# HGRN2 in a hybrid encoder: scores for the diagonal 32x32 chunks alone, and both heads' value and state products ordered by block

## The chip, the cores and the metric

The kernel runs on one core of one Trainium2 chip. The metric is the device time of one execution in microseconds (us). TensorE (PE in the profile) multiplies matrices, and loads its weights on a sequencer of its own (PEld); VectorE is DVE, ScalarE is ACT, GpSimd is POOL, and SyncE (SP) issues most DMAs. Each engine works through its own list of instructions in order and waits on semaphores of the others.

## The reference

Two layers of an encoder over 512 tokens of width 1024. A layer normalizes, projects once, runs four mixers on column groups of the projection (Hyena, Mamba2, dilated attention, HGRN2), projects out, and ends in a mixture of 16 experts. The change is in HGRN2, which runs once per direction e (forward, backward), four heads of 64 channels each, in chunks of 32 tokens:

```python
def gla_chunked(q, k, v, g):
    q, k, v, g = rs(q), rs(k), rs(v), rs(g)             # (batch, chunk, 32, head, channel)
    gc = jnp.cumsum(g, axis=2)
    ref = gc[:, :, H_CHUNK // 2 - 1:H_CHUNK // 2]
    scores = jnp.einsum("bclhe,bcshe->bchls", q * jnp.exp(gc - ref), k * jnp.exp(ref - gc))
    scores = jnp.where(jnp.tril(jnp.ones((32, 32), bool)), scores, 0.0)
    o_intra = jnp.einsum("bchls,bcshp->bclhp", scores, v)
    U = jnp.einsum("bclhe,bclhp->bchep", k * jnp.exp(g_last - gc), v)
    _, prev = lax.scan(step, S0, (U, a))                # S = a * S + U, chunk by chunk
    o_inter = jnp.einsum("bclhe,bchep->bclhp", q * jnp.exp(gc), prev)
    return o_intra + o_inter
```

So a token meets only the tokens of its own chunk through a score, and all earlier chunks through the state `prev`. With 512 tokens there are 16 chunks, hence 16 blocks of 32x32 scores per head and direction.

## The kernel before

A layer's mixers are Python generators. `weave` (L428) advances two of them by turns, in proportion to the numbers that they yield, and so makes the program order; from that order a scheduler sets each engine's list when the program is built. In each layer `hgrn` is woven with `mamba_proj` (L584): while HGRN2 waits for a vector engine, TensorE does the projection of the Mamba mixer, `pcm` (128x128 weights, 512 columns, L395 to L397) and `ptm` (L417 to L419).

`hgrn` (L1119) works on heads in pairs: i is the pair, h the head in it, and head h's 64 channels lie on partitions 64h to 64h+63. For a pair, `hgrn_decay` makes the decayed keys and queries `gqk` and the decayed queries for the states `gqi`, for both directions e. Then, per direction, keys are transposed (`gkT`, L1135), multiplied with the values (`gU`, L1143, 64x64 weights), copied by ACT (L1148, L1150), and VectorE runs the scan over the 16 chunks (`gR`, L1153 or L1155, 128x1024).

Then comes the part that the change touches, per head h:

- Scores. For each direction four products of 128x128 (L1164): the tokens are taken 128 at a time (block b), though only the four 32x32 blocks on the diagonal are wanted. Weights have 64 rows and 128 columns.
- Mask. GpSimd clears a tile `gP` (L1166, 128x512), VectorE copies the wanted elements into it under a mask (`copy_predicated`, L1167, 128x512). After both directions VectorE adds the two tiles (L1170).
- Products. Per block b one product of the masked scores with the values (L1173, 128x128 weights, 64 columns), and then, for each chunk cc of the block and each direction, one product of decayed queries with the state (L1180, weights of 64 rows and 32 columns, 64 moving columns). All accumulate in the PSUM bank `go` of that head: `pov[h][:, b, i]`, chunk cc on partitions 32cc to 32cc+31.

A product of float32 operands leaves two records in the trace (two passes, each with its own load of weights). Per pair that makes 16 score products (32 passes), 8 value products (16 passes) and 60 state products (120 passes); there are two pairs in each of two layers.

After both pairs: squares on ACT (`gsq`, L1189), sums on VectorE (`gss`, L1190), the norm, a transposition on TensorE (`gyT`, L1202).

Of the kernel before, what the change touches and what calls it, by code (L numbers as in the profile page):

```python
# [20 lines left out]
P = 128  # L21
# [17 lines left out]
def shape_constants():  # L39
    f32 = np.float32  # L40
    p = np.arange(P)
    c = np.zeros((P, C_N), f32)
    c[:, C_ID:C_ID + P] = np.eye(P)
    c[:, C_LE:C_LE + P] = p[:, None] <= p[None, :]
    c[:, C_GE:C_GE + P] = p[:, None] >= p[None, :]
    c[:, C_IOTA:C_IOTA + 64] = np.arange(1, 65)
    c[:, C_TOK:C_TOK + 4] = 2 * (P * np.arange(4)[None, :] + p[:, None])
    c[:, C_HALF] = p >= 64
    c[:, C_KEY] = 1.0 / KEY
    c[:, C_KEY + 1] = 1.0  # L50
    c[:, C_SLOT] = p % 64 + 1
    same = (p[:, None] // 32) == (p[None, :] // 32)
    m = np.zeros((P, 2, P), np.int32)
    m[:, 0] = same & (p[:, None] <= p[None, :])
    m[:, 1] = same & (p[:, None] >= p[None, :])

    eo = np.concatenate([np.arange(0, L, 2), np.arange(1, L, 2)])
    f = 2.0 * np.pi * (np.arange(P, dtype=np.float64) + 0.5) / (2 * L)  # L60
    n = np.arange(L).reshape(P, 4).T
    th = n[:, :, None] * f
    dft = np.stack([np.cos(th), np.sin(th)]).astype(f32)
    idft = np.ascontiguousarray(dft.transpose(0, 1, 3, 2))
    tk = [eo[:, None] * f, eo[:, None] * (np.pi / 2 - f)]
    kdft = np.stack([np.concatenate([np.cos(tk[0]), np.cos(tk[1])], axis=1),
                     np.concatenate([np.sin(tk[0]), -np.sin(tk[1])], axis=1)])
    kdft = (kdft * (2.0 / (2 * L))).astype(f32)

    t = np.linspace(0.0, 1.0, L, dtype=f32)[:, None]  # L70
    ang_pos = (f32(2.0 * math.pi) * np.arange(L, dtype=f32) / f32(L)).astype(f32)
    bands = np.linspace(1e-4, 15, 16, dtype=f32)
    ang = (ang_pos[:, None] * bands[None, :]).astype(f32)
    z = np.concatenate([t, np.cos(ang), -np.sin(ang)], axis=-1).astype(f32)
    lo = math.log(1e-2) / 1.5
    hi = math.log(1e-2) / 0.3
    deltas = np.abs(np.linspace(lo, hi, 256, dtype=f32))
    decay = np.exp(-t * deltas[None, :]).astype(f32)[eo]

    d = np.arange(511, -512, -1)  # L80
    n = np.abs(d)
    nf = np.maximum(n, 1).astype(f32)
    large = 8 + (np.log(nf / f32(8)) / f32(math.log(128.0)) * f32(8)).astype(np.int32)
    bucket = (d > 0) * 16 + np.where(n < 8, n, np.minimum(large, 15))
    mult = (n <= 64).astype(int) + ((n <= 256) & (n % 4 == 0)) + (n % 16 == 0)
    oh = np.zeros((33, 1024), f32)
    oh[bucket, np.arange(1023)] = 1.0
    oh[32, :1023] = np.where(mult > 0, np.log(np.maximum(mult, 1)), -1e30)
    return {
        "c_pack": c, "c_hmask": m, "c_dft": dft, "c_idft": idft, "c_kdft": kdft,  # L90
        "c_zT": np.ascontiguousarray(z.T), "c_decay": decay, "c_bucket": oh,
    }
# [18 lines left out]
def encoder(ctx: ExitStack, tc: tile.TileContext, d, out, dbg=None, stages=None, nlayers=NL):  # L111
# [35 lines left out]
    def bank_b(name):  # L147
        return tagged(psb, "b", [512], F32, name)
# [71 lines left out]
    ps = bank_b("nmT")  # L220
# [898 lines left out]
    def hgrn(l, st, cols, lb):  # L1119
# [9 lines left out]
        for i in range(2):  # L1129
            qk, qi, bes = yield from hgrn_decay(l, i, q, f, lb, keep)  # L1130
            R = [tl("B", [64, 16], "gR") for _ in range(2)]
            for e in range(2):
                ps = bank_b("gkT")
                for b in range(4):
                    T.transpose(ps[:, b * P:(b + 1) * P], qk[1][:, e, b * P:(b + 1) * P], ident)  # L1135
                kT = page([4, P], "gkT")
                A.activation(kT, ps.rearrange("p (b c) -> p b c", b=4), AF.Copy)
                pu = [bank_b("gU") for _ in range(2)]
                for b in range(4):
                    for z in range(2):  # L1140
                        a = slice(64 * z, 64 * z + 64)
                        for h in range(2):
                            T.matmul(pu[z][64 * h:64 * h + 64, b * P:(b + 1) * P], kT[a, b, 64 * h:64 * h + 64],  # L1143
                                     ve[b][a, 2 * i + h], start=True, stop=True)

                U, w = tl("B", [64, 16], "gU"), tl("B", [64, 16], "gw")
                for z in range(2):
                    A.activation(U.rearrange("p n (b z c) -> p z b c n", z=2, c=2)[:, z],  # L1148
                                 pu[z].rearrange("p (b c n) -> p b c n", b=4, n=64), AF.Copy)
                A.activation(w, bes[e][:, None, :].to_broadcast([P, 64, 16]), AF.Copy)  # L1150
                u, r, w = (x.rearrange("p n c -> p (n c)") for x in (U, R[e], w))
                if e == 0:
                    V.tensor_tensor_scan(r, w, u, 0.0, ALU.mult, ALU.add)  # L1153
                else:
                    V.tensor_tensor_scan(r[:, ::-1], w[:, ::-1], u[:, ::-1], 0.0, ALU.mult, ALU.add)  # L1155
                yield 2.5
            for h in range(2):
                s = slice(64 * h, 64 * h + 64)
                Ps = []
                for e in range(2):  # L1160
                    ps = bank_b("gsc")
                    for b in range(4):
                        c = slice(b * P, (b + 1) * P)
                        T.matmul(ps[:, c], qk[1][s, e, c], qk[0][s, e, c], start=True, stop=True)  # L1164
                    w = page([4, P], "gP")
                    G.memset(w, 0.0)  # L1166
                    V.copy_predicated(w, hmask[:, e, None, :].to_broadcast([P, 4, P]),  # L1167
                                      ps.rearrange("p (b c) -> p b c", b=4))
                    Ps.append(w)
                V.tensor_add(Ps[0], Ps[0], Ps[1])  # L1170
                yield 2
                for b in range(4):
                    T.matmul(pov[h][:, b, i], Ps[0][:, b], v[:, b, (2 * i + h) * 64:(2 * i + h + 1) * 64],  # L1173
                             start=True, stop=False)
                    for cc in range(4):
                        c = 4 * b + cc
                        for e in range(2):
                            p = c - 1 if e == 0 else c + 1
                            if 0 <= p < 16:
                                T.matmul(pov[h][32 * cc:32 * cc + 32, b, i], qi[s, e, 32 * c:32 * c + 32],  # L1180
                                         R[e][s, :, p], start=False, stop=(e == 1 or c == 15))
                    yield 0.8
        gs = tl("B", [4, 256], "ggs")
        silu_inplace(g, gs, gs)
        y = tl("B", [4, 256], "gy")
# [457 lines left out]
```

## Time and profile before

| | before |
|---|---|
| runs, us (median of 3) | 1653.99 (1653.51 to 1654.05) |
| profiled execution, us | 1657.14 |
| its span, first to last instruction, us | 1655.4 |
| PE busy | 1531.7 us, 93% of the span |
| DVE busy | 802.6 us, 48% |
| ACT busy | 396.1 us, 24% |
| POOL busy | 213.8 us, 13% |
| mean granted TensorE clock | 0.971 |

All times in rows are in us from the start of the span, unless marked ns. The profiled execution lies 3.15 us above the median of the runs. `hgrn` of layer 0 fills the stretch from about 102 to 183 us, that of layer 1 from about 920 to 995 us. Matmuls are pipelined, so the rate of a burst is read from starts: a row of the timeline merges like instructions, its start is that of the first and its length ends with the last one's modelled end.

### The profile page before, as it was taken

What the parts mean: (1) busy time and instruction counts of PE and PEld (TensorE: products, weight loads), DVE (VectorE), ACT (ScalarE), POOL (GpSimd) and SP (SyncE); (2) the same over time, 40 slices, a digit from 0 to 9 for tenths busy, and PEclk for the clock granted to TensorE, in tenths of its full rate; (3) what the DMA queues carried; (4) which work ended last, traced back from release to release, by engine and by line L of the source; (5) the groups of instructions that cost most, each with busy time, mean ns of one, the idle gap of its engine ahead of it and who ended that gap; (6) DMA issues with size and microseconds to landing.
All of it is one profiled execution on the core that took longest, in us unless ns stands there. A gap on an engine that the chain in (4) does not pass through costs nothing.

```text
span 1655.4 us, 22757 instructions
## 1 busy us (share of the span) xinstructions
PE 1531.7 (93%) x8899; PEld 880.2 (53%) x8899; DVE 802.6 (48%) x1727; ACT 396.1 (24%) x805; POOL 213.8 (13%) x214
## 2 busy tenths in 40 slices
PE   6989998989999998989979999999899999998985
PEld 5778787763433432334368788787434433332332
DVE  6777677573333331432256767856533333332323
ACT  4344333431000000001162435243200001000012
POOL 3232133000000000000033232310000000000001
PEclk9989899999999999999989889999899999999998
DMA  5411223679999999999932202167799999999996
GB/s 169 127 51 36 68 77 141 239 288 341 421 420 421 421 420 399 421 420 420 419 95 82 72 27 77 54 233 266 262 407 418 420 422 420 421 420 421 420 420 247
DMA packets 153773, 468.54 MB, mean 283 GB/s; under 512 B 20440, under 2 KB 56696, under 8 KB 144962
## 3 DMA queue, kind: packets, MB, share of 16 engines
q1 hardware_dynamic: 145030, 455.10, 70.3%
q0 software_dynamic: 2240, 7.34, 1.1%
q10 hardware_dynamic: 6396, 4.65, 0.8%
q8 instruction: 70, 1.15, 0.3%
q14 instruction: 37, 0.30, 0.0%
HBM read 460.60 MB, written 6.44 MB: 282 GB/s over the span
## 4 chain that ended last, share of the span: by engine, by line
PE 63%; DMA 25%; DVE 6%; ACT 3%; issue 2%; POOL 1%; ACTq 0%; SPq 0%; DVEq 0%; POOLq 0%
PE eg L1404 9%; DMA we<-in_moe_w_up_dram 9%; DMA we<-in_moe_w_down_dram 9%; PE eu L1404 8%; PE ey L1404 7%; DMA we<-in_moe_w_gate_dram 5%; PE pcm L395 3%; PE pcm L396 3%; PE pcm L397 3%; PE ec L1475 2%; PE po L1222 2%; PE po L1223 2%; PE po L1224 2%; PE ptm L418 2%; PE ptm L417 2%
## 5 line engine op out<-in xcount | busy, mean ns | idle before, releaser
L1404 PE MATMUL eu<-we,exT 128*64 128x512 f32 x1024 | 237.9, 598 | 17.2 <-DMA we<-in_moe_w_up_dram 14.9
L1404 PE MATMUL ey<-we,ehT 128*64 128x512 f32 x1024 | 233.1, 600 | 17.3 <-ACT ehT L1440 11.2
L1404 PE MATMUL eg<-we,exT 128*64 128x512 f32 x1024 | 230.7, 598 | 10.4 <-DMA we<-in_moe_w_gate_dram 6.4
L1404 PEld LDWEIGHTS eu<-we,exT 128*64 128x64 f32 x1024 | 67.7, 136 | 181.6 <-issue 91.9
L1303 DVE SCALAR_TENSOR_TENSOR ra<-er,ra,tie 128x512 bf16<-128x512 f32 x128 | 95.9, 749 | 128.6 <-PE er L1311 125.7
L1404 PEld LDWEIGHTS ey<-we,ehT 128*64 128x64 f32 x1024 | 70.2, 137 | 155.5 <-issue 102.1
L1404 PEld LDWEIGHTS eg<-we,exT 128*64 128x64 f32 x1024 | 69.2, 136 | 149.6 <-issue 111.5
L1457 DVE SCALAR_TENSOR_TENSOR eY<-ey,erg,eY 64x512 fp32r<-64x512 f32 x64 | 48.0, 750 | 189.2 <-ACT eY L1456 189.1
L1425 ACT ACTIVATE eh<-eg 128x512 f32<-128x512 f32 x32 | 19.1, 598 | 498.6 <-PE eg L1404 498.6
L397 PE MATMUL pcm<-hT,whl 128*128 128x512 f32 x320 | 128.9, 403 | 3.5 <-DVE whl L381 3.5
L1476 DVE TENSOR_TENSOR x<-x,ec 128x512 f32<-128x512 f32 x128 | 81.0, 691 | 102.6 <-PE ec L1475 102.5
L396 PE MATMUL pcm<-hT,whl 128*128 128x512 f32 x320 | 130.2, 407 | 0.0
L395 PE MATMUL pcm<-hT,whl 128*128 128x512 f32 x320 | 129.9, 406 | 0.0
L1348 POOL DMA_INDIRECT exe<-xd,erow x28 | 27.8, 994 | 787.0 <-DVE erg L1329 660.1
L1456 ACT ACTIVATE eY<-ey,erg 64x512 fp32r<-64x512 f32 x64 | 43.7, 683 | 268.3 <-PE ey L1404 243.9
L1432 DVE TENSOR_TENSOR eh<-eh,eu 128x512 f32<-128x512 f32 x32 | 22.0, 687 | 153.9 <-PE eu L1404 153.9
L417 PE MATMUL ptm<-wtm,hT 128*128 128x256 f32 (+1 forms) x256 | 76.1, 298 | 1.7 <-DVE aqs L926 1.7
L1475 PE MATMUL ec<-eY,eot 128*128 128x512 f32 x256 | 67.3, 405 | 10.2 <-DVE erow L1346 6.4
L418 PE MATMUL ptm<-wtm,hT 128*128 128x256 f32 (+1 forms) x256 | 74.2, 291 | 1.3 <-DVE wtm L381 1.3
L380 POOL TENSOR_SCALAR whl<-wraw 128x1024 fp32r<-128x1024 f32 x40 | 46.9, 1173 | 220.1 <-PE pcm L397 127.7
L419 PE MATMUL ptm<-wtm,hT 128*128 128x256 f32 (+1 forms) x256 | 72.8, 288 | 0.0
L397 PEld LDWEIGHTS pcm<-hT,whl 128*128 128x128 f32 x320 | 62.3, 195 | 18.2 <-DVE whl L381 3.9
(394 smaller groups left out, 2374.8 us busy)
## 6 DMA issues: line engine op xcount, KB each, us to landing
we<-in_moe_w_gate_dram SPq DMA_DIRECT2D x218, 512.0 KB
we<-in_moe_w_up_dram SPq DMA_DIRECT2D x208, 512.0 KB
we<-in_moe_w_down_dram SPq DMA_DIRECT2D x206, 512.0 KB
wraw<-in_w_in_dram SPq DMA_DIRECT2D x27, 1024.0 KB
we<-in_moe_w_down_dram SPq DMA_DIRECT2D x25, 1024.0 KB
we<-in_moe_w_up_dram SPq DMA_DIRECT2D x24, 1024.0 KB
we<-in_moe_w_gate_dram SPq DMA_DIRECT2D x19, 1024.0 KB
wo<-in_w_out_dram SPq DMA_DIRECT2D x8, 1024.0 KB
```

Of the source, the lines that this page charges most:

```text
L380: G.tensor_scalar(dst_hi, raw, 1.0, 0.0, op0=ALU.mult, op1=ALU.add)
L395: T.matmul(ps, w[:, 0, k, :], H[k], start=(k == 0), stop=False)
L396: T.matmul(ps, w[:, 0, k, :], Lo[k], start=False, stop=False)
L397: T.matmul(ps, w[:, 1, k, :], H[k], start=False, stop=(k == 7))
L417: T.matmul(dst, h, w[:, 0, k % 4], start=(k == 0), stop=False)
L418: T.matmul(dst, h, w[:, 1, k % 4], start=False, stop=False)
L419: T.matmul(dst, g, w[:, 0, k % 4], start=False, stop=(k == 7))
L1303: V.scalar_tensor_tensor(g, pr, ra[:, c, e, 0:1], tie[:, 384 - c * P:896 - c * P], op0=ALU.subtract, op1=ALU.is_gt, accum_out=k)
L1404: T.matmul(ps[f][64 * f:64 * f + 64], xT[:, j, h], qs[4 * h + j][:, f * 512:(f + 1) * 512], start=(h == 0 and j == 0), stop=(h == 1 and j ...
L1457: V.scalar_tensor_tensor(lo, src, w[c, 0:1], hi.bitcast(F32), op0=ALU.mult, op1=ALU.subtract)
L1475: T.matmul(ps, ot[:, t * P:(t + 1) * P], Y[i][q][n], start=(q == 0), stop=(q == 1))
L1476: V.tensor_add(xrow(t)[:, c], xrow(t)[:, c], ps)
```

## The change

In the mask constant both directions now hold one 32x32 triangle, repeated for four column blocks and four row blocks. `hgrn` takes both heads of a pair together:

```diff
@@ shape_constants @@
-    same = (p[:, None] // 32) == (p[None, :] // 32)
-    m = np.zeros((P, 2, P), np.int32)
-    m[:, 0] = same & (p[:, None] <= p[None, :])
-    m[:, 1] = same & (p[:, None] >= p[None, :])
+    m = np.zeros((P, 2, 4, 32), np.int32)
+    m[:, 0] = ((p % 32)[:, None] <= np.arange(32))[:, None]
+    m[:, 1] = ((p % 32)[:, None] >= np.arange(32))[:, None]
+    m = m.reshape(P, 2, P)
@@ hgrn @@
+            pc = [bank_b("gsc") for _ in range(2)]
+            for e in range(2):
+                for c in range(16):
+                    b, cc = divmod(c, 4)
+                    t = slice(32 * c, 32 * c + 32)
+                    for h in range(2):
+                        s = slice(64 * h, 64 * h + 64)
+                        T.matmul(pc[h][32 * cc:32 * cc + 32, P * e + 32 * b:P * e + 32 * b + 32], qk[1][s, e, t],
+                                 qk[0][s, e, t], start=True, stop=True)
+            w = page([2, 2, P], "gP")
+            G.memset(w, 0.0)
             for h in range(2):
-                s = slice(64 * h, 64 * h + 64)
-                Ps = []
-                for e in range(2):
-                    ps = bank_b("gsc")
-                    for b in range(4):
-                        c = slice(b * P, (b + 1) * P)
-                        T.matmul(ps[:, c], qk[1][s, e, c], qk[0][s, e, c], start=True, stop=True)
-                    w = page([4, P], "gP")
-                    G.memset(w, 0.0)
-                    V.copy_predicated(w, hmask[:, e, None, :].to_broadcast([P, 4, P]),
-                                      ps.rearrange("p (b c) -> p b c", b=4))
-                    Ps.append(w)
-                V.tensor_add(Ps[0], Ps[0], Ps[1])
-                yield 2
-                for b in range(4):
-                    T.matmul(pov[h][:, b, i], Ps[0][:, b], v[:, b, (2 * i + h) * 64:(2 * i + h + 1) * 64],
-                             start=True, stop=False)
+                V.copy_predicated(w[:, h], hmask, pc[h][:, :256].rearrange("p (e c) -> p e c", e=2))
+            V.tensor_add(w[:, :, 0], w[:, :, 0], w[:, :, 1])
+            yield 3
+            for b in range(4):
+                for h in range(2):
+                    for cc in range(4):
+                        t = slice(32 * cc, 32 * cc + 32)
+                        T.matmul(pov[h][t, b, i], w[t, h, 0, 32 * b:32 * b + 32],
+                                 v[t, b, (2 * i + h) * 64:(2 * i + h + 1) * 64], start=True, stop=False)
+                for h in range(2):
+                    s = slice(64 * h, 64 * h + 64)
                     for cc in range(4):
...
-                    yield 0.8
+                yield 1.2
```

Per pair there are now 64 score products (weights of 64 rows and 32 columns, 32 moving columns; 128 passes), 32 value products (32x32 weights, 64 columns; 64 passes), and the same 60 state products (120 passes). VectorE has two masked copies of 128x256 and one addition of 128x256 in place of four copies and two additions of 128x512; GpSimd clears one tile of 128x512 in place of four.

TensorE's list in layer 0, pair 0, before. `gU` ends the chunk products, `gsc` are scores, `pcm` is the Mamba projection, `go` takes values (from `gv`) and states (from `gR`):

```order
L1143 MATMUL gU_1079<-gve_895,gkT_1076 64x128 x2
L1164 MATMUL gsc_1102<-gqk_956,gqk_957 128x128 x4
L1164 MATMUL gsc_1110<-gqk_956,gqk_957 128x128 x4
L396 MATMUL pcm_1125<-hT_127,whl_1122 128x512
...
L1173 MATMUL go_954<-gv_260,gP_1107 128x64
L1164 MATMUL gsc_1195<-gqk_956,gqk_957 128x128 x3
L1180 MATMUL go_954<-gR_1039,gqi_958 32x64
L1180 MATMUL go_954<-gR_1038,gqi_958 32x64
...
L1173 MATMUL go_954<-gv_260,gP_1107 128x64
L1180 MATMUL go_954<-gR_1038,gqi_958 32x64
```

The same place after the change:

```order
L1143 MATMUL gU_1079<-gve_895,gkT_1076 64x128 x2
L1165 MATMUL gsc_1102<-gqk_956,gqk_957 32x32
L1165 MATMUL gsc_1103<-gqk_956,gqk_957 32x32
...
L396 MATMUL pcm_1179<-hT_127,whl_1176 128x512
...
L1177 MATMUL go_954<-gv_260,gP_1168 32x64 x4
L1177 MATMUL go_955<-gv_260,gP_1168 32x64 x4
L1186 MATMUL go_954<-gR_1039,gqi_958 32x64
L1186 MATMUL go_954<-gR_1038,gqi_958 32x64
...
L1186 MATMUL go_955<-gR_1039,gqi_958 32x64
```

The second head's scores and products, which stood behind another 24 `pcm`, now stand with the first head's: 64 scores in a row, 14 `pcm`, then four blocks, each of 8 values and 28 or 32 state passes per head. In pair 1 of both layers the four blocks stand two and two, with 16 or 24 `ptm` between them, and before `gyT` there are 25 `pcm` (before 23 in layer 0, 26 in layer 1).

VectorE's list in layer 1, pair 0, before (`gR` is the scan, `ge` belongs to the next pair's decay):

```order
L1153 SCALAR_TENSOR_TENSOR gR_6840<-gw_6868,gU_6867 128x1024
L449 TENSOR_TENSOR mu_6712<-mu_6712,me_6835 128x512
L1167 COPY_PREDICATED gP_6909<-hmask,gsc_6904 128x512
L1167 COPY_PREDICATED gP_6917<-hmask,gsc_6912 128x512
L1155 SCALAR_TENSOR_TENSOR gR_6841<-gw_6899,gU_6898 128x1024
L1170 TENSOR_TENSOR gP_6909<-gP_6909,gP_6917 128x512
L1085 TENSOR_TENSOR ge_7091<-gl_7090,ge_7091 128x512
```

And after:

```order
L1153 SCALAR_TENSOR_TENSOR gR_6962<-gw_6990,gU_6989 128x1024
L449 TENSOR_TENSOR mu_6834<-mu_6834,me_6957 128x512
L1170 COPY_PREDICATED gP_7092<-hmask,gsc_7026 128x256
L1155 SCALAR_TENSOR_TENSOR gR_6963<-gw_7021,gU_7020 128x1024
L1170 COPY_PREDICATED gP_7092<-hmask,gsc_7027 128x256
L1085 TENSOR_TENSOR ge_7274<-gl_7273,ge_7274 128x512
L1171 TENSOR_TENSOR gP_7092<-gP_7092 128x2x128
```

The second masked copy now stands behind the second scan, and one operation of the next pair ahead of the addition.

## Rows read from the trace of the kernel before

**Rows 1.** The page, chain that ended last: shares of the span by engine.
```profile
PE 63%; DMA 25%; DVE 6%; ACT 3%; issue 2%; POOL 1%; ACTq 0%; SPq 0%; DVEq 0%; POOLq 0%
```

**Rows 2.** Busy time by stretch: PE, PEld, DVE, ACT, POOL, clock, DMA, GB/s.
```profile
102.00:183.00 81.00, 73.61 (x675) 61.20 (x674) 59.61 (x95) 34.85 (x55) 21.65 (x25) 0.83 0.14 40
920.00:995.00 75.00, 69.65 (x658) 57.96 (x658) 54.14 (x87) 32.75 (x51) 19.32 (x17) 0.84 0.10 29
```

**Rows 3.** Waits of PE (total us, times, longest), three stretches: 85:200, 900:1010, 190:345.
```profile
PE gU L1143 <- ACT gkT L1137: 7.1, 2, 6.3
...
PE go L1173 <- DVE gP L1170: 3.8, 2, 2.7
...
PE pcm L397 <- DVE whl L381: 1.7, 1, 1.7
```

**Rows 4.** Groups by line, PE, whole span: count | busy us, mean ns | idle before.
```profile
L1164 PE MATMUL gsc<-gqk,gqk 64*128 64x128 f32 x128 | 23.6, 354 | 0.0
L1180 PE MATMUL go<-gR,gqi 64*32 64x64 f32 x480 | 21.3, 291 | 0.0
L1324 PE MATMUL ers<-ra 128*64 128x3 f32 x512 | 19.6, 198 | 0.0
L1173 PE MATMUL go<-gv,gP 128*128 128x64 f32 x64 | 15.9, 337 | 4.1 <-DVE gP L1170 4.1
```

**Rows 5.** Timeline of PE, layer 0, full clock: start, length, count of passes.
```profile
136.96 0.65 PE L1180 MATMUL go<-gR,gqi 64*32 64x64 f32 x16
137.53 0.43 PE L1173 MATMUL go<-gv,gP 128*128 128x64 f32 x2
137.90 0.66 PE L1180 MATMUL go<-gR,gqi 64*32 64x64 f32 x16
...
152.66 2.05 PE L1164 MATMUL gsc<-gqk,gqk 64*128 64x128 f32 x16
154.64 0.39 PE L417 MATMUL ptm<-wtm,hT 128*128 128x264 f32 x1
```

**Rows 6.** Timeline of PE, layer 1, half clock.
```profile
935.08 0.69 PE L1180 MATMUL go<-gR,gqi 64*32 64x64 f32 x16
...
936.32 0.69 PE L1180 MATMUL go<-gR,gqi 64*32 64x64 f32 x16
...
938.16 3.78 PE L1164 MATMUL gsc<-gqk,gqk 64*128 64x128 f32 x16
```

**Rows 7.** Chain that ended last, layer 1: start, length, engine and line.
```profile
931.75 1.39 DVE gP L1170
...
943.09 0.43 PE pcm L395
...
947.59 0.23 PE pcm L396
```

**Rows 8.** Timeline of PE: a burst of products with three moving columns.
```profile
373.07 0.63 PE L1324 MATMUL ers<-ra 128*64 128x3 f32 x16
```

**Rows 9.** Busy time in the stretches of half clock, columns as in rows 2.
```profile
113.40:123.60 10.20, 9.27 (x57) 7.94 (x58) 9.04 (x13) 7.55 (x13) 0.00 (x0) 0.50 0.00 0
161.20:178.20 17.00, 17.00 (x118) 13.64 (x118) 8.93 (x26) 2.41 (x7) 0.00 (x0) 0.50 0.21 63
932.60:946.20 13.60, 12.93 (x94) 10.70 (x95) 10.35 (x17) 3.91 (x7) 0.60 (x1) 0.50 0.01 1
973.50:983.80 10.30, 10.30 (x71) 8.51 (x63) 6.97 (x17) 1.06 (x3) 0.00 (x0) 0.50 0.07 7
```

**Rows 10.** Groups by line, DVE, 90 to 1000 us.
```profile
L1167 DVE COPY_PREDICATED gP<-hmask,gsc 128x512 f32<-128x512 uint8 x16 | 11.5, 735 | 10.4 <-PE gsc L1164 9.5 <-POOL gP L1166 0.9
...
L692 DVE TENSOR_SCALAR mz<-ptm 128x256 f32<-128x256 f32 x8 | 3.3, 413 | 0.2
```

**Rows 11.** Timeline of PE at the end of layer 1's HGRN2.
```profile
987.89 0.65 PE L1180 MATMUL go<-gR,gqi 64*32 64x64 f32 x14
...
994.50 1.03 PE L1202 MATMUL gyT<-pk,gy 128*128 128x128 f32 x8
```

## The prediction

> **What bounds the kernel now.** I read the chain of waits first: PE carries 63% of the span and DMA 25% [rows 1]; the DMA part is expert weights in the second half of each layer. In the two HGRN2 stretches DMA is nearly idle and PE is busy 73.6 of 81 us and 69.7 of 75 us [rows 2]. So there the time is PE's list: a pass saved is time saved, so long as the work behind it is ready. Second, PE's waits: in the stretch of layer 1 it stood 3.8 us for the masked scores `gP`, in layer 0 it stood 7.1 us for the key copies `gkT`, and in the stage behind HGRN2 its longest wait is 1.7 us [rows 3]. An earlier end of HGRN2 therefore passes on almost whole, through the mixers and to the weight DMAs, whose buffers the mixers release. Third, the granted clock: 51.1 us of the two stretches run at 0.50, the lower level of 1.2 GHz [rows 9].
>
> **Where the time of the changed part goes.** Scores, states and values are 23.6 + 21.3 + 15.9 = 60.8 us of PE in both layers [rows 4]. The reader should see three prices. (1) A score block of 16 passes takes 154.64 - 152.66 = 1.98 us at full clock [rows 5], 124 ns a pass, and 3.78 us at half [rows 6]; it scales with the clock. (2) A block of 16 state passes lasts 0.65 us of which the last pass is 0.29 (mean, rows 4): (0.65 - 0.29) / 15 = 24 ns a pass at full clock [rows 4, 5], (0.69 - 0.29) / 15 = 27 ns at half [rows 4, 6]. It hardly scales. (3) The last state starts at 136.96 + 0.65 - 0.29 = 137.32, the next value at 137.53: 0.21 us, and from that value to the next state 0.37 us for two passes [rows 4, 5]. A change between weights of 64x32 and of 128x128 costs about 0.21 us where a pass inside a block costs 0.024: some 0.18 extra.
>
> **The price of the new small products.** No row shows weights of 64x32 with 32 columns or of 32x32. The nearest are the state passes at 24 to 27 ns with 64 columns, and a burst with only 3 moving columns, 16 passes in 0.63 us with a last one of 0.198: 29 ns [rows 4, 8]. Twenty times fewer columns are no faster, so a small pass seems to cost its issue and not its columns. I take 27 ns for every small pass, at either clock. Ends: 29 ns above. Below, if all eight positions (two heads, four chunks) overlapped and only streaming counted: a score pass of 128 columns is 124 ns [rows 5], 32 columns are 31 ns, over eight positions 4 ns.
>
> **The sum.**
> - Scores: 4 pairs x 128 = 512 passes x 0.027 = 13.8 us. That is what 32 passes of 124 ns a pair cost now at full clock (15.9): narrower scores gain little there. The gain is at half clock, where the old blocks are twice as long.
> - Values and states: 4 pairs x 184 = 736 passes x 0.027 = 19.9 us, and 16 blocks with two changes of shape each, 32 x 0.18 = 5.8 us (before 64 changes in 32 blocks). Together 25.7 us for today's 37.2.
> - 60.8 - 13.8 - 25.7 = 21.3 us gained.
> - Half clock: a value and state block takes 936.32 - 935.08 = 1.24 us there, 137.90 - 136.96 = 0.94 at full [rows 5, 6], 0.30 more for two changes. If half of the 16 new blocks fall there: 8 x 0.3 = 2.4 us back.
> - Full-width work at half clock: a `pcm` takes 0.43 us there and 0.23 at full [rows 7]. Of the 51.1 us at half clock I count four score blocks (15), three heads' products (15) and 3 for idle and chunk products; the rest is some 42 `pcm`, which lose 42 x 0.2 = 8.4 us. I leave that as it is; ends: none of it lost (8.4 gained) or twice as much.
> - VectorE: four copies of 735 ns and two additions become three operations of half the size, about 0.41 each by the nearest 128x256 row [rows 10], some 3 us a pair less. DVE is busy 54 to 60 us in these stretches [rows 2], so this counts only where PE waits. GpSimd's three clearings fewer count nothing: POOL is busy a quarter of the stretch [rows 2].
> - Waits for `gP`: 4.1 us before [rows 4]. In layer 1, pair 0, the addition follows the second scan and ended its wait at 931.75 + 1.39 = 933.14 [rows 7]; in the new list a masked copy and one operation stand between (about 0.4 + 0.7), with the addition shorter. PE arrives later, as 128 passes take 3.5 us for 2.0 and 14 `pcm` stand there for 12. I expect some 1.4 us of wait here and 0.5 in layer 0: 2.2 us gained.
> - End of HGRN2: PE runs 26 `pcm` from 987.89 + 0.65 to `gyT` at 994.50 without a wait [rows 11]. Now both heads end together: one more square and one more sum, each about 0.7 as another operation on 128x512 [rows 10], behind 25 `pcm`. Up to 1.3 us a layer, 2.6 us lost.
> - The next pair's chain: PE arrives some 3 us earlier at `gkT` and `gU`, which wait for ACT's copies; it already stood 7.1 us there [rows 3]. Bounds 0 and 7 us; I take 3.5 lost, half, as VectorE's shorter list speeds part of that chain.
> - 21.3 - 2.4 + 2.2 - 2.6 - 3.5 = 15.0 us.
>
> Against the profiled execution that is a span of 1655.4 - 15 = 1640.4 and a time of 1657.14 - 15 = 1642; the runs' median is 3.15 us lower than the profiled one, so I forecast 1654 - 15 = 1639.
>
> **Rivals.**
> 1. *The low clock stays longer.* The clock fell to 1.2 GHz at 161.2 and at 973.5 just after value and state blocks, at 113.4 and 932.6 after PE had idled [rows 3, 9]. Now both heads' blocks stand in a row, some 6.4 us a pair by the prices above in place of 3.7. If all four such runs draw a low stretch as long as the longest seen (17 us, about half of it full-width work), the full-width loss is 4 x 17 / 2 / 2 = 17 us for 8.4, and all 16 blocks pay 0.3, 2.4 more: 11 of the 15 us are gone, 1650. [...] Against: the products around 137 us drew no fall [rows 5], and there are half as many bursts.
> 2. *The value products queue up, slower.* In each block four products of 32 rows, at four row positions, write one PSUM bank `pov[h]`. Elsewhere the kernel gives each row position its own bank (`pu[z]`, and the scores' `pc[h]`), so no row shows this case. If each value product waits until the one before has left, as at a change of shape (0.21 us, rows 5), 128 of them cost 128 x (0.21 - 0.054) = 20 us more: 1659. It decides for slower from 0.054 + 15 / 128 = 0.17 us a product. Against it: the four write different partitions. The Trainium skill, "TensorEngine Tiling (Array Packing)", Restrictions and Gotchas, says that different row tiles cannot access the same PSUM bank at once; by that rule this rival would hold, and no run here shows it yet.
> 3. *Small products overlap fully.* At the lower end, 4 ns a score pass, the scores cost 2 us and not 13.8; the values gain perhaps 2 more: 14 us better, 1625. Against it stand the 29 ns for three columns [rows 8]. The Trainium skill, "TensorE: Matmul & The Clock Gate", Part 3, counts about 4 ns for each further tile of a packed group; by that the sum would be this one, and rows 5 and 8, with 24 and 29 ns, speak against it.
>
> That the change does not do what it says I leave out: TensorE's list shows the small products, in blocks with both heads.
>
> **How the numbers follow.** Forecast (gain 8 to 23 us, its own range 1631 to 1646): 0.56. Rival 1: 0.18, some 0.08 of it still faster by over 0.2%, 0.10 not. Rival 2: 0.12. Rival 3: 0.07. The rest, 0.07, is for small losses that I have not priced and that eat the gain, mostly to no change. A measurement of this kernel can tell about 0.2%, 3.3 us, from no change. So faster 0.71, same 0.15, slower 0.14. For the range I leave out most of rival 2 above and most of rival 3 below: 1627 to 1655.
>
> **What would show it.** Right: scores of a pair as one burst of about 3.5 us at either clock; a block of 46 passes about 1.6 us, with 0.2 us at its two changes of shape; two value groups of four as fast as states (8 products in about 0.4 us); PE's waits for `gP` near 2 us in sum, a new wait before `gyT` of a microsecond. Wrong: value products 0.17 us apart or more (rival 2); more than 51 us at clock 0.50 in the two stretches (rival 1); score passes well under 20 ns (rival 3); or PE's waits at `gkT` and `gU` grown by the whole gain.

## The result and the profile after

The changed kernel takes 1629.6 us (median of four runs, 1627.11 to 1630.68) beside 1654.02 us of the kernel before on the same chip: a ratio of 0.9833, with an interval of 0.9806 to 0.9861 (the two medians alone give 0.9852). The forecast was 1639. The time lies inside the range of 1627 to 1655, near its lower end, but the gain is 24.4 us by the medians where 15.0 were forecast, just outside the forecast's own 8 to 23. In the profiled executions 1657.14 became 1630.68, with spans of 1655.4 and 1628.9 us.

The page of the changed kernel, busy time of PE and the chain that ended last (in the kernel before, PE had 63% of the chain, DVE 6% and "issue" 2% [rows 1]):

```profile
PE 1499.7 (92%) x9475; PEld 854.3 (52%) x9475; DVE 789.8 (48%) x1715; ACT 394.0 (24%) x805; POOL 212.2 (13%) x202
...
PE 59%; DMA 23%; DVE 8%; issue 4%; ACT 3%; POOL 2%; ACTq 0%; SPq 0%; DVEq 0%; POOLq 0%
```

PE's groups by line, as in [rows 4]. States, values and scores were 21.3, 15.9 and 23.6 us:

```profile
L1186 PE MATMUL go<-gR,gqi 64*32 64x64 f32 x480 | 11.5, 290 | 0.0
...
L1177 PE MATMUL go<-gv,gP 32*32 32x64 f32 x256 | 8.1, 237 | 6.4 <-DVE gP L1171 5.4 <-issue 1.0
...
L1165 PE MATMUL gsc<-gqk,gqk 64*32 64x32 f32 x512 | 6.6, 223 | 1.9 <-issue 1.3 <-ACT gU L1148 0.5
```

PE's timeline, to be read beside [rows 5, 6]: a pair's scores in layer 0 (at half clock) and in layer 1 (at full clock), and two blocks of values and states of both heads:

```profile
118.76 1.55 PE L1165 MATMUL gsc<-gqk,gqk 64*32 64x32 f32 x128
...
946.17 1.51 PE L1165 MATMUL gsc<-gqk,gqk 64*32 64x32 f32 x128
...
128.13 0.43 PE L1177 MATMUL go<-gv,gP 32*32 32x64 f32 x16
128.49 0.72 PE L1186 MATMUL go<-gR,gqi 64*32 64x64 f32 x32
129.14 0.43 PE L1177 MATMUL go<-gv,gP 32*32 32x64 f32 x16
```

The reader should see the rates. 128 score passes last 1.51 us, of which the last takes about 0.22: (1.51 - 0.22) / 127 = 10 ns a pass, and the same at half clock. A block holds 16 value passes and 28 or 32 state passes for both heads together, so 14 or 16 states per head and not 28 or 32. A block of 48 passes for both heads repeats after 129.14 - 128.13 = 1.01 us; before, one head's block of 18 passes took 0.94.

PE's waits in 85:200 and 900:1010, as in [rows 3]:

```profile
PE gU L1143 <- ACT gkT L1137: 9.4, 2, 6.2
PE go L1177 <- DVE gP L1171: 2.3, 1, 2.3
PE gyT L1208 <- DVE gy L1203: 0.7, 1, 0.7
...
PE go L1177 <- DVE gP L1171: 3.1, 2, 2.2
PE gsc L1165 <- issue: 1.3, 1, 1.3
```

Busy time in the stretches of half clock inside HGRN2, columns as in [rows 9], where they made 51.1 us; now 20.5:

```profile
115.80:122.60 6.80, 5.75 (x166) 4.88 (x167) 6.47 (x11) 5.75 (x10) 0.00 (x0) 0.50 0.01 2
149.90:156.80 6.90, 6.37 (x161) 5.84 (x154) 4.50 (x9) 5.81 (x6) 0.00 (x0) 0.51 0.01 2
924.80:931.60 6.80, 6.25 (x172) 4.50 (x157) 6.80 (x12) 1.98 (x5) 0.00 (x0) 0.50 0.02 5
```

**The account.** To compare kernels I take, per layer, the stretch from the first key transposition `gkT` to the first product of the next stage (`mcb`): before, 102.80 to 196.57 and 917.87 to 1007.57. The view of busy time by stretch ends with a sum over both: the length, then each engine's busy time. PE's idle time is the length less PE's busy time. Of the kernel before, in this order: all work, then the instructions of the tiles `gsc` (scores), `go` (values and states) and `pcm` (full-width projection) alone:

```profile
sum 183.47, PE 170.72 PEld 138.85 DVE 137.24 ACT 76.44 POOL 44.16; mean PE 85.36 PEld 69.42 DVE 68.62 ACT 38.22 POOL 22.08
...
sum 183.47, PE 23.58 PEld 21.45 DVE 11.53; mean PE 11.79 PEld 10.72 DVE 5.77
...
sum 183.47, PE 33.34 PEld 24.93 DVE 2.58 ACT 2.39; mean PE 16.67 PEld 12.46 DVE 1.29 ACT 1.19
...
sum 183.47, PE 69.76 PEld 50.21 DVE 25.96 ACT 7.41; mean PE 34.88 PEld 25.10 DVE 12.98 ACT 3.71
```

The same four of the changed kernel:

```profile
sum 155.48, PE 134.13 PEld 107.65 DVE 124.60 ACT 75.11 POOL 41.29; mean PE 67.06 PEld 53.83 DVE 62.30 ACT 37.56 POOL 20.64
...
sum 155.48, PE 6.56 PEld 5.73 DVE 3.25; mean PE 3.28 PEld 2.86 DVE 1.62
...
sum 155.48, PE 17.75 PEld 12.18 DVE 2.56 ACT 2.17; mean PE 8.88 PEld 6.09 DVE 1.28 ACT 1.09
...
sum 155.48, PE 61.62 PEld 45.49 DVE 25.95 ACT 7.42; mean PE 30.81 PEld 22.75 DVE 12.97 ACT 3.71
```

The two stretches lost 28.0 us; 1.5 came back elsewhere. The first stretch began 2.5 us later than before (105.32 for 102.80), behind some 7 us at half clock near 70 us that the profile before does not have.

PE's busy time fell by 170.72 - 134.13 = 36.6 us, and PE's idle time took back 8.6 (183.47 - 170.72 = 12.75 before, 21.35 after). By tiles, scores gave 17.0, values and states 15.6, and `pcm` 8.1 without one product fewer. That is 40.7; the rest of the list, with the tails that a sum by tiles counts twice, took 4.1 back.

Each kernel's stretches are read from one execution. Where a kernel was profiled twice, the sums differ by up to 1.7 us: 155.48 and 157.10 for the change, 156.40 and 157.01 for in_turn, 154.81 and 156.48 for turn_spread. A smaller step than that is no finding.

### The profile page after: what moved, and what is told of

It reads as the page before. It is cut to its first block, busy times and chain, and to the rows that moved or that the text cites. A ratio compares the mean times of both kernels' runs of the same rounds, so it can differ in the third digit from the quotient of the medians.

```text
span 1628.9 us, 23876 instructions
## 1 busy us (share of the span) xinstructions
PE 1499.7 (92%) x9475; PEld 854.3 (52%) x9475; DVE 789.8 (48%) x1715; ACT 394.0 (24%) x805; POOL 212.2 (13%) x202
## 4 chain that ended last, share of the span: by engine, by line
PE 59%; DMA 23%; DVE 8%; issue 4%; ACT 3%; POOL 2%; ACTq 0%; SPq 0%; DVEq 0%; POOLq 0%
PE eg L1410 10%; DMA we<-in_moe_w_down_dram 9%; PE ey L1410 8%; PE eu L1410 8%; DMA we<-in_moe_w_up_dram 8%; DMA we<-in_moe_w_gate_dram 5%; PE pcm L397 3%; PE pcm L395 3%; PE pcm L396 3%; PE ec L1481 2%; PE po L1228 2%; PE po L1229 2%; PE po L1230 2%; PE apv L992 1%; PE ptm L418 1%
## 5 line engine op out<-in xcount | busy, mean ns | idle before, releaser
L1431 ACT ACTIVATE eh<-eg 128x512 f32<-128x512 f32 x32 | 19.1, 598 | 496.6 <-PE eg L1410 496.6
```

## The experiments

A position of the array is here the 64 rows of one head and the 32 columns of one chunk of a block: eight in all. The first theory (overlap): passes at different positions run beside each other, so they cost less than the 27 ns that the prediction took. Its rivals: fewer microseconds at 1.2 GHz (clock), the shorter masks (VectorE), and taking the heads together, so that there is less waiting (order).

### One part alone in the kernel before

**scores_only**: narrow scores in the old banks.

```diff
-  T.matmul(ps[:, c], qk[1][s, e, c], qk[0][s, e, c], start=True, stop=True)
+  for cc in range(4):
+      t = slice(b * P + 32 * cc, b * P + 32 * cc + 32)
+      T.matmul(ps[32 * cc:32 * cc + 32, t], qk[1][s, e, t], qk[0][s, e, t], start=True, stop=True)
...
```

> The kernel before with one part of the change: 64 score products of 32x32 in place of 16 of 128x128, written at the diagonal of the same four banks; masks by four copies of 32 rows each; values, states and the order of the heads as before. Overlap (the passes on different positions of the array run beside each other, 10 to 14 ns a pass where the prediction took 27): scores fall from 23.6 us of PE to 5 to 8 us, and the time by 10 to 16 us against before. The prediction's price (27 ns): scores 14 us, time 5 to 9 us shorter. Clock (the extra gain came from fewer us at 1.2 GHz): under 6 us shorter, and the stretches at 0.50 shrink first. Order (taking both heads together made the gain): 0 to 3 us.

Measured: ratio 0.9953 (0.9933 to 0.9974), about 8 us (5.9 by the medians): in the 5 to 9 of the prediction's price and under the 10 to 16 of overlap. Yet PE's scores fell as overlap says, from 23.58 to 8.10 us in the two stretches, but those became only 5.4 us shorter. The kernel has a flaw of its own: the 64 copies of 32 rows cost VectorE 19.1 us where 16 copies cost 11.5, and PE's waits for `gP` rose from 4.1 to 8.4. Its stretches also hold seven more `pcm` than before. It shows the price of the passes, and not what they are worth in time.

**values_only**: four 32x32 value products for one of 128x128.

```diff
-  T.matmul(pov[h][:, b, i], Ps[0][:, b], v[:, b, ...], start=True, stop=False)
+  for cc in range(4):
+      t = slice(32 * cc, 32 * cc + 32)
+      T.matmul(pov[h][t, b, i], Ps[0][t, b, t], v[t, b, ...], start=True, stop=False)
```

> The kernel before with one part of the change: four value products of 32x32 weights per block in place of one of 128x128; scores, masks, states and the order of the heads as before. Overlap: a value group of 8 passes lasts 0.1 us in place of two passes of 0.16, the change of shape to the states shortens from 0.21 to 0.14: 0.12 to 0.2 us for each of 32 blocks, 4 to 6 us shorter. One bank, one product at a time (rival 2): 128 products at 0.17 us, 10 us longer or more. Order: no change.

Measured: 0.9932 (0.9910 to 0.9955), about 11 us, twice what was expected. Values and states gave the 5.9 us foreseen (33.34 to 27.43). The rest is read as clock: half clock inside HGRN2 fell from 51.1 to 30.8 us, and with it `pcm` by 3.1 us and the unchanged scores by 1.7. The executions agree: the median granted clock of ten is 0.977 (0.972 to 0.979), of those before beside them 0.972 (0.967 to 0.975); scores_only had 0.969.

**pairs_only**: both heads side by side with the old scores, masks and values.

```diff
+  Pw.append(Ps[0])              # scores and masks of both heads first
...
+  for b in range(4):
+      for h in range(2):        # values of both heads
...
+      for h in range(2):        # then states of both heads
```

> The kernel before with one part of the change: both heads' scores, then per block both heads' values and both heads' states; scores 128x128, masks and values 128x128 as before. Overlap: the states of the second head run beside those of the first (14 ns a pass for 24): 960 passes x 10 ns = 9.6 us, and 32 changes of shape fewer, 0.15 each, 4.8 us; less some 2 to 4 us of longer waits for four masks in a row: 8 to 13 us shorter. The prediction's prices (states 24 to 27 ns whatever the order): 2 to 5 us shorter. Order (the gain is from fewer waits): PE's busy time in states stays near 21 us while the time falls.

Measured: 0.9952 (0.9935 to 0.9970), about 8 us (6.4 by the medians). The expectation counts 960 state passes where there are 480, so its first term is 4.8 us and not 9.6, and its range for overlap some 3 to 8. Where the second head's masks came late, the scheduler set blocks of one head alone in front, so states fell only from 21.3 to 18.1 us. The sums of its unchanged scores and of `pcm` show where most of its time came from:

```profile
sum 172.68, PE 18.00 PEld 16.81 DVE 11.07; mean PE 9.00 PEld 8.40 DVE 5.54
...
sum 172.68, PE 65.38 PEld 47.98 DVE 25.91 ACT 7.46; mean PE 32.69 PEld 23.99 DVE 12.95 ACT 3.73
```

Of the 10.8 us by which its stretches shrank, values and states gave 3.5 (33.34 to 29.83). The same scores took 5.6 us less and the same `pcm` 4.4, as less of this execution's HGRN2 ran at half clock. So the kernel does half of what was meant, and it does not tell order and clock apart.

### One part undone: the heads in turn

**in_turn** is the changed kernel with one loop over h around scores, mask and products, as before the change:

```diff
-  pc = [bank_b("gsc") for _ in range(2)]
+  for h in range(2):
+      ps = bank_b("gsc")        # 32 narrow scores, compact mask, values and states of this head
...
-      yield 1.2
+          yield 0.8
```

> The kernel after the change with the heads in turn again: narrow scores, compact masks and 32x32 values, but the second head's scores and products behind the first's, at the place they had before. Overlap: scores and values keep their gain (some 15 and 4 us), states go back to 24 ns a pass (21 us of PE for 11.5) and 32 changes of shape come back: 12 to 17 us shorter than before, 8 to 13 us longer than the change. Order: within 5 us of before. Scores and values alone (states do not matter): within 4 us of the change.

Measured: 0.9837 (0.9810 to 0.9865): as fast as the change, against what overlap said. Its sums, in the same order:

```profile
sum 156.40, PE 142.30 PEld 111.35 DVE 126.26 ACT 76.51 POOL 41.77; mean PE 71.15 PEld 55.67 DVE 63.13 ACT 38.25 POOL 20.89
...
sum 156.40, PE 8.55 PEld 7.25 DVE 3.51; mean PE 4.27 PEld 3.63 DVE 1.75
...
sum 156.40, PE 27.75 PEld 17.56 DVE 2.58 ACT 2.39; mean PE 13.88 PEld 8.78 DVE 1.29 ACT 1.20
...
sum 156.40, PE 63.11 PEld 45.73 DVE 25.92 ACT 8.17; mean PE 31.55 PEld 22.87 DVE 12.96 ACT 4.09
```

The 10 us of values and states came back (27.75 for 17.75), just as expected, the scores were 2.0 us dearer, and PE's idle time fell by 7.3 in exchange (14.10 for 21.35). So the side-by-side order saves PE 10 us that are not on the path that sets the end.

### The order of the passes alone

**by_position**: the same 512 score passes, those of one position in a row.

```diff
-  for e in range(2):
-      for c in range(16):
-          b, cc = divmod(c, 4)
-          for h in range(2):
+  for h in range(2):
+      for n in range(32):
+          cc, e, b = n // 8, n // 4 % 2, n % 4
...
```

> The kernel after the change with the same 512 score passes in another order: all 16 passes that use one position of the array (head h, chunk cc) in a row, then the next position; nothing else differs. Overlap by position: passes at one position cannot run beside each other, 32 columns at the old rate of 124 ns for 128 are 31 ns a pass, so scores take about 14 us of PE from start to start for 6.3, and the time grows by 4 to 8 us against the change. Cheap passes in any order (12 ns is only the rate of issue): scores stay at 6 to 7 us and the time within 2 us of the change.

Its first burst in layer 0 (half clock) and in layer 1 (full clock):

```profile
116.23 5.72 PE L1165 MATMUL gsc<-gqk,gqk 64*32 64x32 f32 x128
...
918.64 3.54 PE L1165 MATMUL gsc<-gqk,gqk 64*32 64x32 f32 x128
```

(3.54 - 0.22) / 127 = 26 ns a pass at full clock, 43 ns at half, where the spread order has 10 ns at both. The same products at the same place: this shows the overlap, and that the prediction's 27 ns is the price of passes which follow each other at one position. The time hardly noticed: 1632.11 us, 0.9851 (0.9822 to 0.9881), with 11.9 us more of scores (18.41):

```profile
sum 161.00, PE 144.60 PEld 119.08 DVE 126.28 ACT 75.22 POOL 40.82; mean PE 72.30 PEld 59.54 DVE 63.14 ACT 37.61 POOL 20.41
...
sum 161.00, PE 18.41 PEld 17.92 DVE 3.58; mean PE 9.21 PEld 8.96 DVE 1.79
```

Again idle time gave way (16.40 for 21.35): of 11.9 us of passes 5.5 reached the length of the stretches.

**states_spread** (direction outermost, head innermost) and **turn_spread** (heads in turn, direction outermost, values first in blocks 0 and 2 and last in blocks 1 and 3):

```diff
-  for cc in range(4):
-      for e in range(2):
+  for e in range(2):
+      for cc in range(4):
```

> The kernel after the change with the same state products in another order: head innermost, then chunk, direction outermost, so that successive products use all eight positions by turns. Overlap by position: states fall from 14 ns a pass to 7 to 10 ns, 4 to 7 us less of PE; of the time 0 to 4 us, since PE already waits there for ACT and VectorE. Issue (14 ns is the rate of issue): no change in states, the time within 2 us of the change.

> The kernel with the heads in turn (narrow scores, compact masks, 32x32 values), and in each head's products the direction outermost, so that successive state products use four positions by turns, and values first in blocks 0 and 2, last in blocks 1 and 3, so that 64 changes between values and states become some 32. Overlap by position: states fall from 24 ns a pass to 12 to 16 (8 us less of PE), changes of shape by 28 x 0.15 = 4 us; the time 4 to 10 us shorter than with the heads in turn, if the waits for ACT and VectorE do not take it. If they do, as they took the 8 us that the two heads side by side save: within 3 us of the change.

Measured: states_spread 0.9841 (0.9814 to 0.9868), states 10.7 us for 11.5; turn_spread 0.9815 (0.9791 to 0.9840), 1626.11 us, states 18.1 for 21.1. Both orders moved the states far less than overlap by position says. A run of 30 state passes in turn_spread:

```profile
124.83 1.11 PE L1182 MATMUL go<-gR,gqi 64*32 64x64 f32 x30
```

That is (1.11 - 0.29) / 29 = 28 ns a pass, though it goes round four positions. So for states it is the second head that halves the price, and not the chunk. The second head uses other rows of the array and another PSUM bank; no run separates the two.

### VectorE's share

**old_masks**: each masked copy four times.

```diff
+  for _ in range(4):
       V.copy_predicated(w[:, h], hmask, pc[h][:, :256].rearrange("p (e c) -> p e c", e=2))
```

> The kernel after the change with each masked copy made four times (the same elements again), so that VectorE works about 3.7 us a pair ahead of the addition as before the change, in place of 1.2; PE's work is that of the change. VectorE (the shorter masks are part of the gain): PE's waits for the masked scores grow from 5.4 to 12 to 15 us and the time by 5 to 10 us against the change. Passes and clock (the masks are hidden): the time within 2 us of the change.

Measured: 0.9817 (0.9790 to 0.9843), not slower than the change. VectorE's copies rose from 3.2 to 11.4 us, as much as before the change, and PE's waits for `gP` were 2.9 us. The shorter masks are no part of the gain.

### The clock

**fill** (on the change) and **turn_fill** (on turn_spread) give PE eight products whose result nobody reads, where it otherwise stands for the second key copy:

```diff
+  if l == 0 and i == 0 and e == 1:
+      for _ in range(8):
+          T.matmul(po[0], ident, qk[1][:, 0], start=True, stop=True)
```

> The kernel after the change with eight products whose result nobody reads (128x128 weights, 512 columns, into the still empty bank of the values) in layer 0, pair 0, where TensorE otherwise stands some 6 us for the second key copy; nine of the Mamba projection's products, 2 us, that stood ahead of that wait move behind the scores. Clock (the low stretch of 7 to 14 us that begins in or behind this wait comes from the standstill, and full-width work in it costs double): the stretch at 0.50 around 110 to 125 us goes away, pcm and chunk products there gain 3 to 5 us, and the time is 1 to 3 us shorter than the change in spite of the 2 us moved. Passes alone (the clock falls for another reason): the stretch stays, and the time is 2 us longer than the change.

> The kernel with the heads in turn and the states spread (turn_spread), and the same eight idle products in layer 0, pair 0. Clock: the low stretch at 111 to 121 us goes, 1 to 3 us shorter than turn_spread. Otherwise: the stretch stays and the time is 2 us longer.

Measured: 0.9866 (0.9839 to 0.9892) and 0.9863 (0.9835 to 0.9891), 1636 us both. In fill the low stretch behind the wait went, as the clock theory says; the next one began at 131.3, within a new standstill of PE (126.57 to 135.18). Busy time of fill by stretch:

```profile
105.00:131.30 26.30, 20.10 (x254) 13.27 (x252) 22.80 (x31) 15.24 (x26) 11.73 (x9) 1.00 0.14 41
131.30:138.20 6.90, 3.02 (x108) 2.32 (x108) 4.46 (x7) 2.28 (x5) 6.20 (x5) 0.51 0.01 2
```

And its waits of PE, 85:200:

```profile
PE go L1180 <- DVE gP L1174: 8.6, 1, 8.6
```

So in this kernel the fall that followed the standstill was gone with it, and one fell in the new standstill. The gain did not come, because the edit also moved ACT's list: the second `gU` copies came at 128.72 (119.62 in the change), the scan behind them on VectorE at 131.40 (123.37), the masks behind the scan, and PE stood 8.6 us for them. That is a price of this edit, not of the clock.

### The waits

**long_gap** (on the change) and **gap_spread** (the same with spread states and the changed order of values):

```diff
-  yield 3
+  yield 8 if i == 0 else 3
```

> The kernel after the change with 8 in place of 3 in the yield behind pair 0's masks, so that 35 products of the projection stand between scores and values where there were 14, and the four blocks of both pairs stand in one row. Waits (what the two heads side by side save in passes is given back in PE's waits for the masked scores): the 4.5 us of waits for the masked scores of pair 0 go, and the time is 2 to 5 us shorter than the change. Waits only move on (PE then arrives earlier at a later copy): the waits for the key copies or for the states grow by as much, and the time stays within 2 us of the change.

> The same longer gap, with the states of both heads spread over eight positions and the values first in blocks 0 and 2, last in blocks 1 and 3, so that 32 changes of shape between values and states become some 20. Overlap: states 2 us and changes 2 us less of PE than the change. If PE bounds the stretch once the gap is longer: 4 to 9 us shorter than the change. If the copies and masks bound it: within 2 us of long_gap.

Measured: 0.9837 (0.9809 to 0.9866) and 0.9828 (0.9802 to 0.9855): no change in either. Groups of long_gap on PE:

```profile
L1143 PE MATMUL gU<-gve,gkT 64*64 64x128 f32 x256 | 10.6, 313 | 13.7 <-ACT gkT L1137 13.7
...
L1177 PE MATMUL go<-gv,gP 32*32 32x64 f32 x256 | 7.6, 231 | 7.2 <-DVE gP L1171 4.7 <-issue 2.4
```

The wait for the key copies is 13.7 us where the change has 10.5: the wait moved on. gap_spread, with another 3 us less of values and states (PE's groups 9.5 and 6.6), gains nothing by them either. What PE waits for is seen in the changed kernel's chain through 105 to 135 us of layer 0, 45 pieces, none of them on PE (start, length, engine; some of them):

```profile
108.10 0.67 DVE mu L712
...
113.65 1.81 ACT gU L1148 x2
...
116.35 2.29 DVE gR L1153
...
124.04 2.69 POOL gqk L1114
```

In the kernel before, 43 of the 63 pieces from 102.8 to 135 us are PE's. Behind 140 us the chain of the changed kernel has a piece of 19.6 us that names nothing, so it is read no further.

### Both prices as forecast

Neither undone part alone made the kernel slower by its passes. **turn_by_position** undoes both: in_turn with the scores of one position in a row. With it ran the change, in_turn and turn_spread once more, on one chip. The edit against in_turn:

```diff
-  for e in range(2):
-      for c in range(16):
-          b, cc = divmod(c, 4)
+  for cc in range(4):
+      for n in range(8):
+          e, b = n // 4, n % 4
...
```

> The kernel with the heads in turn, and its scores ordered by position as in by_position: 16 passes of one position in a row. So neither the scores nor the states run beside others: scores at the prediction's 27 ns a pass at full clock, states and changes of shape at the prediction's prices. Passes are the missed terms, and either of the two savings alone fills the time until the chain of copies and masks sets the end: with both taken away the stretch from the first key transposition to the next stage loses 8 to 12 us of the 27 gained, and the time is 1636 to 1641, near the forecast. Something else is the missed term (the clock, or VectorE's shorter work): the time stays within 3 us of in_turn.

> The changed kernel once more, with the others of this comparison on the same chip: 0.983 of before, as a scale for the other three. Its low stretches of the clock may lie elsewhere than in the first profile.

> The kernel with the heads in turn once more, beside the change on the same chip. If the two heads side by side are worth nothing in time: within 3 us of the change. If they are worth their 8 us of passes: 5 us longer or more.

> Heads in turn with states spread over four positions and fewer changes of shape, once more, beside the change and in_turn on the same chip. If PE's passes still bound the heads in turn: 2 us shorter than in_turn or more. If the copies and masks do: within 2 us of it.

Measured: turn_by_position 1635.04 us, 0.9870 (0.9839 to 0.9900); change_again 1629.77, 0.9844 (0.9815 to 0.9873); in_turn_2 1630.23, 0.9838 (0.9810 to 0.9866); turn_spread_2 1628.05, 0.9834 (0.9802 to 0.9865). The heads side by side are worth nothing that can be measured, and no version beats the change by more than the intervals allow. Sums of turn_by_position:

```profile
sum 162.66, PE 151.37 PEld 120.64 DVE 127.14 ACT 76.49 POOL 43.53; mean PE 75.68 PEld 60.32 DVE 63.57 ACT 38.24 POOL 21.77
...
sum 162.66, PE 17.47 PEld 16.31 DVE 3.56; mean PE 8.73 PEld 8.16 DVE 1.78
...
sum 162.66, PE 27.61 PEld 17.45 DVE 2.58 ACT 2.39; mean PE 13.80 PEld 8.72 DVE 1.29 ACT 1.20
...
sum 162.66, PE 64.00 PEld 46.29 DVE 25.95 ACT 8.13; mean PE 32.00 PEld 23.14 DVE 12.98 ACT 4.07
```

Its stretches are 6.3 us longer than those of in_turn and 7.2 longer than the change's, a little less than the 8 to 12 expected. By the ratios the step to in_turn is 0.3%, some 5 us, and the intervals overlap; but on this chip five of the six executions (1633.38 us and more) are longer than every one of in_turn_2 (at most 1631.25). The step is there; its size is the profile's. The parts nearly add up: undone alone they lengthen the stretches by 5.5 us (by_position) and 0.9 (in_turn), together by 7.2.

## Why the prediction was too low

The direction was right, and so was the reason for the kernel before: the time of these stretches was PE's list. The size was not. The two stretches lost 28.0 us; the experiments lay that out in three steps.

- Before to turn_by_position, 183.47 - 162.66 = 20.8 us: the change with passes near the forecast's prices. Of it 5.8 us are `pcm` (69.76 to 64.00), full-width products of which fewer ran at half clock.
- turn_by_position to in_turn, 6.3 us: scores that overlap.
- in_turn to the change, 0.9 us: heads side by side, less than two profiles of one kernel differ by.

Without the `pcm` and the overlap 15.0 us are left, the number forecast, but partly by luck: in turn_by_position scores gained 6.1 us and values and states 5.7, where the forecast had 9.8 and 11.5, and idle time fell by 1.5 where the forecast's waits came to 3.9 more. The terms:

- **The price of the new small products** is the step that failed: "I take 27 ns for every small pass, at either clock". Measured 10 ns for scores and (0.43 - 0.24) / 15 = 13 ns for values. 27 ns is right for passes at one position at full clock (26), but not "at either clock" (43 at half). The reason given, that a pass "seems to cost its issue and not its columns", was drawn from bursts of one head or of full height (rows 5, 6 and 8); the new score burst goes round eight positions, so the lower end (4 ns) was the nearer one. Scores cost 6.6 us, not 13.8.
- **Values and states.** Forecast 25.7, measured 17.75; in_turn with 27.75 shows that the forecast's price was that of heads in turn. With both heads in one block a state costs (0.72 - 0.29) / 31 = 14 ns a pass. In time this was worth nothing that can be measured. The starting sum was too high as well: 21.3 and 15.9 us by line count the tails that lie beside each other twice, 33.34 together.
- **Half clock.** "I leave that as it is" was the second failed step: 51.1 us became 20.5, and `pcm` gained 8.1, the end that the prediction named as 8.4 (change_again has 61.48 for 61.62). This is HGRN2 alone: over the whole kernel the granted clocks of 0.971 and 0.976 make 96 and 78 us at half clock, so the other stages had some 13 us more of it than before. The 2.4 us for blocks at half clock I did not measure apart. What draws a low stretch is seen for the standstill in layer 0 alone (fill). That the two falls behind value and state blocks (161.2 and 973.5) are missing in most kernels with 32x32 values is seen in one profile each, and their cause stays open.
- **Waits.** For `gP` 2.2 us less were forecast; PE came earlier, and they rose from 4.1 to 5.4. `gyT` cost 0.7 and 0.8, forecast 1.3 each. The wait for the key copies rose by 2.6 (9.4 and 1.1 for 7.1 and 0.8), forecast 3.5. Not foreseen: 2.3 us of idle time inside bursts of small passes for which the profile names nothing ("issue"). In all 8.6 us came back as idle time.
- **VectorE** was rightly counted as nothing for the masks (old_masks).

The rivals. The low clock did not stay longer in HGRN2 but less. The value products did not queue up: 16 passes, from four row positions into one bank per head, take 0.43 us, 25 ns a product of two passes where rival 2 asked for 0.17 us or more. The Trainium skill, "TensorEngine Tiling (Array Packing)", Restrictions and Gotchas, says that different row tiles cannot access one PSUM bank at the same time; in this trace they do, each on partitions of its own: sixteen passes of 0.24 us each are done within 0.43 us. Full overlap, 1625 us at a chance of 0.07, came nearest to the time, with 10 ns where it had 4. The Trainium skill, "TensorE: Matmul & The Clock Gate", Part 3, has packed products overlap, at about 4 ns for each further tile. The trace agrees on the overlap (10 ns a score pass); the 4 ns no run here shows as the rate of a burst.

## What to carry to other kernels

A price taken from a burst holds for that burst's places on the array: look whether the new products follow each other at one position or go round several, and whether another head's products stand beside them. Before adding up what PE saves, ask what the chain of the other engines would take without PE: here 36.6 us less of PE's busy time shortened the stretches by 28.0, and the 10 us that the side-by-side order saves turned into idle time. The worth of such a saving was seen only by undoing it and reading the length of the stretch, not the busy time. And full-width work at half clock belongs into the sum as a term of its own, with both ends.

## What had not been expected of the hardware

- The same 128 score passes take 1.5 us in one order and 3.5 (full clock) or 5.7 us (half clock) in another. Spread over positions they cost 10 ns at either clock; at one position 26 ns and 43.
- States, which go to four chunks' positions on the rows of one head, cost 24 ns (one chunk after the other) or 28 ns (round the chunks); only the other head in the same block brought 14.
- Small passes in long bursts meet idle time that no semaphore explains: 1.3 us inside a burst of 128, 2.4 us in long_gap. In in_turn, with bursts of 64, PE's groups of scores, values and states show none worth naming, nor do the 128 slower score passes of by_position. The cause was not tried.
